# Half of a convolution as ScalarE products added by GpSimd, and three more weight blocks split

## The chip, the cores and the metric

One of the eight cores of a Trainium2 chip runs the program. The metric is the device time of one execution, in microseconds (us). The engines of the core work side by side, each through its own queue in order: TensorE (PE in the profile; its weight loads are PEld) multiplies matrices, VectorE (DVE) and ScalarE (ACT) work elementwise on tiles of 128 partitions, GpSimd (POOL) does small elementwise work and issues some transfers, and SyncE (SP) issues the large ones. SBUF holds 128 partitions of data, PSUM holds TensorE's results.

## The reference

A transformer of three layers on one sequence of 256 tokens, width 1024, all in float32. Two layers form the first block (attention mixers, a dense feed-forward and a mixture of experts). The second block, where the change lies, is:

```python
u = rms_norm(h, mix_norm_g)
proj = u @ w_in
q, k, v, glu_a, glu_g = split(proj)            # 512 columns each
attn_out = moba_attention(heads(q), heads(k), heads(v), rel_bias)
c = glu_a * sigmoid(glu_g)
c = depthwise_causal_conv(c, w_dw, taps=31) + b_dw
conv_out = silu(layer_norm(c) * ln_g + ln_b)
h = h + concat([attn_out, conv_out]) @ w_out
h = h + (silu(rms_norm(h) @ w_gate) * (rms_norm(h) @ w_up)) @ w_down
return rms_norm(h, final_norm_g)
```

With 256 tokens there is a single attention block, so attention is causal softmax attention over 256 keys with a bias by distance, eight heads of 64.

## The kernel before: how the work is laid out

The program is one long straight line in the order of the network. All weights stream in blocks of 1 MB, 128 partitions by 2048 columns, through the class `Stream`: a block is loaded into one of a few raw buffers by SyncE (`_load`, L81), and split into a high and a low part (`_split`, L93): ScalarE writes the rounded high part `wh` (L103), VectorE subtracts it from the raw values into `wl` (L104). A product then takes three passes of TensorE in the fast rounded format (`mm3`, L198): high by high, high by low, low by high. There are three raw and three split buffers here. A block whose number is in `native` is not split: TensorE multiplies the raw float32 values directly, which the profile shows as two matmul instructions for each product, and its raw buffer is held until TensorE has read it.

In the second block the ten blocks of `w_in2` are numbered from 0: blocks 0 to 3 hold the gated convolution input, 128 channels each (tile `ct`), with the gate beside its value; 4 and 5 are q, 6 and 7 are k, 8 and 9 are v. `NATIVE2` (L31) names the unsplit ones: 0, 1, 4, 5, 6 and 7. `proj_cols` (L281) computes a block with channels on the partitions, `proj_tok` (L306) with tokens on them.

The convolution (L1279 to L1302): for each of the four channel tiles ScalarE computes the sigmoid of the gate (L1281), VectorE multiplies (L1282) into `ug`. `conv(ct)` (L1292) starts the sum `cv` with the bias and the last tap on ScalarE (L1294) and adds the 30 other taps on VectorE, each a multiply by a weight per partition and an addition, over a shifted range of 226 to 255 columns (L1298):

```python
for j in range(30):
    back = 30 - j
    nc.vector.scalar_tensor_tensor(cv[:, ct, back:], ug[:, ct, :T - back], cw[:, ct, j:j + 1],
                                   cv[:, ct, back:], op0=ALU.mult, op1=ALU.add)
```

Attention runs in four steps (`STEPS`: two token halves, two groups of four heads). `scores` (L460): TensorE's products of q and k into two PSUM banks, on VectorE the bias and the row maximum (L481) and its negation (L483), on ScalarE the exponential with its sum (L485), on VectorE the reciprocal (L487), on ScalarE the scaling (L490). `values` (L495): transposes (L501), ScalarE copies (L504), the product with v, and the split of the result into `oT` (L204, L205). Each of the first two steps is followed by one block of v, whose PSUM bank (number 7) ScalarE empties (L1305).

After the last tap: the mean over channels by TensorE (`pmu`), VectorE's subtraction (L1326), ScalarE's square (L1327), the variance by TensorE (`pvr`, L1333), GpSimd's reciprocal root (`rstd_of`, L345), a product that spreads it over the partitions (`prs`), VectorE's multiplication (L1343), ScalarE's SiLU (L1345) and the split. The product with `w_out2` (four blocks) is cut into eight parts of 12 matmuls (token half by weight block, `Mix.part`, L527); the parts of blocks 2 and 3 need the convolution, those of 0 and 1 attention.

The order of each engine's queue is set when the program is built, by a planner: among the instructions whose inputs are ready by its own estimates it takes the one that stands first in the program, and `high_priority` sections ahead of the others. The splits of `w_in2` are such a section. `tc.issue_after(x)` keeps an instruction behind `x` in its engine's queue. On the chip each queue then runs in that fixed order, each instruction waiting for its semaphores. GpSimd also scales the factors of the next norm by 32 (`times32`, L231) and issues small loads (`load_small`, L215).

Of the kernel before, what the change touches and what calls it, by code (L numbers as in the profile page):

```python
# [10 lines left out]
F32 = mybir.dt.float32  # L11
# [4 lines left out]
AF = mybir.ActivationFunctionType  # L16
ALU = mybir.AluOpType
AX = mybir.AxisListType

P = 128  # L20
D = 1024
T = 256
# [5 lines left out]
NE = 8  # L28
R_RAW = 3
N_SPLIT = 3  # L30
NATIVE2 = (0, 1, 4, 5, 6, 7)  # L31


class Buffers:
# [109 lines left out]
def tile_model(ctx, tc, io, out):  # L144
    nc = tc.nc
# [22 lines left out]
    for i in range(len(steps_) + 1):  # L168
        if i < len(steps_):
            e, j = steps_[i]  # L170
            moe_order += [io[n][e][j][kh] for n in ("w1_m", "w3_m") for kh in range(2)]
        if i:
            e, j = steps_[i - 1]
# [107 lines left out]
    def proj_cols(xT, full=None, group="mm"):  # L281

        wh, wl = take8()
        o = bank(group, "pc")
        for ct in range(2):
            for k in range(8):
                oc = o[:, ct * 256:(ct + 1) * 256]
                if wl is None:
                    mm(oc, wh[:, k, tok(ct)], full[:, k, :], k == 0, k == 7)
                else:  # L290
                    mm3(oc, wh[:, k, tok(ct)], wl[:, k, tok(ct)], xT[0][:, k, :], xT[1][:, k, :], k == 0, k == 7)
        return o.rearrange("p (c t) -> p c t", c=2)
# [272 lines left out]
    xT = new_xT()  # L565
# [9 lines left out]
    with tc.tile_pool(name="l0", bufs=1) as lp:  # L575
# [6 lines left out]
        qT = lp.tile([P, 4, T], F32, tag="qT", name="qT")  # L582
        kT = lp.tile([P, 4, T], F32, tag="kT", name="kT")
        vb = lp.tile([P, 2, 512], F32, tag="vb", name="vb")
        with tc.tile_pool(name="gla", bufs=1) as gp:
# [35 lines left out]
            for tt in range(2):  # L621
# [3 lines left out]
                for q in range(2):  # L625
# [5 lines left out]
                    for j in range(2):  # L631
                        rl = g2([P, 2, 256], "rl")
                        nc.scalar.activation(rl[:, :, :S], pis[j][:, :, :S], AF.Relu)
                        for i in range(2):
# [3 lines left out]
                                                           op0=ALU.mult, op1=ALU.add)  # L638
                            first = False
                for r in range(8):  # L640
# [4 lines left out]
                                               op0=ALU.not_equal, op1=ALU.max)  # L645
# [76 lines left out]
            for tt in range(2):  # L722
# [13 lines left out]
                for h in range(4):  # L736
                    nc.vector.scalar_tensor_tensor(o_s[:, h, :], o_s[:, h, :], rs[:, h:h + 1], sg[:, tt, tok(h)],
                                                   op0=ALU.mult, op1=ALU.mult)
# [9 lines left out]
        with tc.tile_pool(name="t0", bufs=1) as tp, tc.tile_pool(name="t0w", bufs=2) as wo:  # L748
# [25 lines left out]
            xT = xT2  # L774
# [3 lines left out]
    with tc.tile_pool(name="f0", bufs=2) as fp, tc.tile_pool(name="f0r", bufs=4) as fr, tc.tile_pool(name="f0w", bufs=1) as fw:  # L778
# [13 lines left out]
        x, xT = xn, xT2  # L792
# [62 lines left out]
    with tc.tile_pool(name="l1", bufs=1) as lp:  # L855
# [6 lines left out]
        with tc.tile_pool(name="fox", bufs=1) as gp:  # L862
# [36 lines left out]
            qT = gp.tile([P, 4, T], F32, tag="qT", name="qT")  # L899
# [31 lines left out]
        with tc.tile_pool(name="t1", bufs=1) as tp, tc.tile_pool(name="t1w", bufs=1) as wo:  # L931
# [5 lines left out]
            copied, logits, xTf = [], [], []  # L937
# [47 lines left out]
    with tc.tile_pool(name="moer", bufs=4) as mr, tc.tile_pool(name="moe2", bufs=2) as m2:  # L985
# [229 lines left out]
        xT = new_xT()  # L1215
        xTf = xp.tile([P, 8, T], F32, tag="b8", name="xTf")
# [46 lines left out]
    with tc.tile_pool(name="s1", bufs=1) as lp:  # L1263
# [3 lines left out]
        cw = load_const(lp, "conv_w")  # L1267
        cpar = load_const(lp, "conv_p")
# [6 lines left out]
        ug = lp.tile([P, 4, T], F32, tag="ug", name="ug")  # L1275
        ga = lp.tile([P, 4, T], F32, tag="ga", name="ga")
        cv = lp.tile([P, 4, T], F32, tag="cv", name="cv")
        ws.first = True
        for ct in range(4):  # L1279
            o = convs[ct] if ct < 1 else proj_cols(xT, xTf)  # L1280
            nc.scalar.activation(ga[:, ct, :], o[:, 0, :], AF.Sigmoid)  # L1281
            nc.vector.tensor_tensor(ug[:, ct, :], ga[:, ct, :], o[:, 1, :], op=ALU.mult)  # L1282
        qT = lp.tile([P, 4, T], F32, tag="qT", name="qT")
        kT = lp.tile([P, 4, T], F32, tag="kT", name="kT")
        for i in range(2):
            nc.scalar.activation(qT[:, 2 * i:2 * i + 2, :], proj_cols(xT, xTf), AF.Copy, scale=0.125)
        for i in range(2):
            nc.scalar.activation(kT[:, 2 * i:2 * i + 2, :], proj_cols(xT, xTf), AF.Copy)
        v = lp.tile([P, 2, 512], F32, tag="v", name="v")
        scores, values = attention(t2, t2, qT, kT, v, lambda h: strip[:, h, :], None, oT, 0, on_act=True)  # L1290

        def conv(ct):  # L1292

            nc.scalar.activation(cv[:, ct, :], ug[:, ct, :], AF.Identity, bias=cpar[:, 0, ct:ct + 1],  # L1294
                                 scale=cw[:, ct, 30:31])
            for j in range(30):
                back = 30 - j
                nc.vector.scalar_tensor_tensor(cv[:, ct, back:], ug[:, ct, :T - back], cw[:, ct, j:j + 1],  # L1298
                                               cv[:, ct, back:], op0=ALU.mult, op1=ALU.add)

        for i, step in enumerate(STEPS):
            conv(i)  # L1302
            scores(*step)
            if i < 2:
                nc.scalar.activation(v[:, :, i * 256:(i + 1) * 256], proj_tok(xT, group="pj"), AF.Copy)  # L1305
            if i:
                values(*STEPS[i - 1])
        with tc.tile_pool(name="t2", bufs=1) as tp, tc.tile_pool(name="t2w", bufs=1) as wo:
# [3 lines left out]
            xT = new_xT()  # L1312
# [31 lines left out]
            for ct in range(4):  # L1344
                nc.scalar.activation(cv[:, ct, :], cv[:, ct, :], AF.Silu, bias=cpar[:, 2, ct:ct + 1],  # L1345
                                     scale=cpar[:, 1, ct:ct + 1])
# [159 lines left out]
```

## Time and profile before

| | |
|---|---|
| median of 3 runs | 1835.7 us (1832.89 to 1836.01) |
| the profiled execution | 1834.43 us |
| its span, first to last instruction | 1832.7 us |
| mean granted clock of TensorE, as a share of full speed | 0.987 |
| busy: PE, DVE, ACT, POOL | 1783.2, 1340.8, 1094.9, 93.9 us |

Times in the rows are microseconds from the span's start. In a timeline a row gives start, duration, engine, line, operation, the tile that it writes and those it reads, shapes, how many are merged (x54), and in brackets the idle time before it and what ended that. A duration runs from an instruction's start to its result; the next one can start before it ends, so for merged rows the time divided by the count is the spacing.

### The profile page before, as it was taken

What the parts mean: (1) busy time and instruction counts of PE and PEld (TensorE: products, weight loads), DVE (VectorE), ACT (ScalarE), POOL (GpSimd) and SP (SyncE); (2) the same over time, 40 slices, a digit from 0 to 9 for tenths busy, and PEclk for the clock granted to TensorE, in tenths of its full rate; (3) what the DMA queues carried; (4) which work ended last, traced back from release to release, by engine and by line L of the source; (5) the groups of instructions that cost most, each with busy time, mean ns of one, the idle gap of its engine ahead of it and who ended that gap; (6) DMA issues with size and microseconds to landing.
All of it is one profiled execution on the core that took longest, in us unless ns stands there. A gap on an engine that the chain in (4) does not pass through costs nothing. (4 is left out here: it accounts for less than half of the span.)

```text
span 1832.7 us, 24585 instructions
## 1 busy us (share of the span) xinstructions
PE 1783.2 (97%) x9903; PEld 1510.5 (82%) x9903; DVE 1340.8 (73%) x1365; ACT 1094.9 (60%) x1014; POOL 93.9 (5%) x136
## 2 busy tenths in 40 slices
PE   8999999999999999999999999999999989899998
PEld 7897999898778888888788788787887868789997
DVE  6856444545678888888888888888888978955443
ACT  5454433444567777777777777777777753564442
POOL 1101100010010000000000000000001022010000
PEclk9999999999989999999999999999999999999999
DMA  8453985263379999999999999999999924536530
GB/s 299 161 186 109 399 319 185 69 214 141 119 308 420 383 377 367 381 365 356 380 369 366 372 368 369 371 376 368 364 370 383 392 95 152 207 139 251 188 123 24
DMA packets 75418, 512.50 MB, mean 280 GB/s; under 512 B 8572, under 2 KB 8725, under 8 KB 17312
## 3 DMA queue, kind: packets, MB, share of 16 engines
q1 hardware_dynamic: 66240, 476.15, 68.1%
q0 software_dynamic: 8768, 34.17, 5.0%
q8 instruction: 80, 1.31, 0.3%
q10 hardware_dynamic: 288, 0.52, 0.1%
q14 instruction: 42, 0.34, 0.1%
HBM read 495.57 MB, written 19.96 MB: 281 GB/s over the span
## 5 line engine op out<-in xcount | busy, mean ns | idle before, releaser
L104 DVE TENSOR_TENSOR wl<-wraw,wh 128x2048 fp32r<-128x2048 f32 (+1 forms) x446 | 1012.0, 2286 | 302.4 <-ACT wh L103 300.3
L103 ACT ACTIVATE wh<-wraw 128x2048 fp32r<-128x2048 f32 (+1 forms) x446 | 851.9, 1912 | 467.8 <-issue 135.1
L196 PE MATMUL hh<-wl,eTh 128*128 128x512 f32 x896 | 355.9, 397 | 3.2 <-DVE wl L104 3.2
L196 PE MATMUL hh<-wh,eTh 128*128 128x512 f32 x896 | 355.2, 396 | 0.0
L196 PE MATMUL hh<-wh,eTl 128*128 128x512 f32 x896 | 353.3, 395 | 0.0
L196 PE MATMUL pc<-xTh,wh 128*128 128x256 f32 x944 | 270.6, 287 | 1.1 <-ACT xTh L204 1.1
L196 PE MATMUL pc<-xTl,wh 128*128 128x256 f32 x944 | 269.4, 285 | 0.9 <-DVE xTl L205 0.8
L196 PE MATMUL pc<-xTh,wl 128*128 128x256 f32 x944 | 269.2, 285 | 0.4 <-DVE wl L104 0.4
L196 PEld LDWEIGHTS hh<-wl,eTh 128*128 128x128 f32 x896 | 168.9, 188 | 46.1 <-DVE wl L104 7.8
L196 PEld LDWEIGHTS hh<-wh,eTh 128*128 128x128 f32 x896 | 168.8, 188 | 38.8 <-ACT eTh L204 0.2
L196 PEld LDWEIGHTS hh<-wh,eTl 128*128 128x128 f32 x896 | 168.8, 188 | 37.9
L196 PEld LDWEIGHTS pc<-xTh,wh 128*128 128x128 f32 x944 | 183.1, 194 | 4.3 <-ACT xTh L204 1.5
L196 PEld LDWEIGHTS pc<-xTl,wh 128*128 128x128 f32 x944 | 183.0, 194 | 2.2 <-DVE xTl L205 1.5
L196 PEld LDWEIGHTS pc<-xTh,wl 128*128 128x128 f32 x944 | 182.9, 194 | 0.7 <-DVE wl L104 0.6
L196 PE MATMUL acc<-wl,mah 128*128 128x512 f32 x448 | 180.8, 404 | 0.0
L196 PE MATMUL acc<-wh,mal 128*128 128x512 f32 x448 | 176.7, 395 | 0.3 <-DVE mal L205 0.3
L196 PE MATMUL acc<-wh,mah 128*128 128x512 f32 x448 | 163.5, 395 | 0.5 <-ACT mah L204 0.5
L196 PEld LDWEIGHTS acc<-wh,mah 128*128 128x128 f32 x448 | 84.4, 188 | 20.6 <-ACT mah L204 0.9
L196 PEld LDWEIGHTS acc<-wh,mal 128*128 128x128 f32 x448 | 84.6, 189 | 18.3 <-DVE mal L205 0.8
L196 PEld LDWEIGHTS acc<-wl,mah 128*128 128x128 f32 x448 | 84.4, 188 | 17.7
L196 PE MATMUL pt<-wh,xTh 128*128 128x256 f32 x256 | 74.7, 293 | 2.2 <-ACT v L1305 1.7
L196 PE MATMUL pt<-wl,xTh 128*128 128x256 f32 x256 | 73.5, 288 | 0.0
(338 smaller groups left out, 1865.7 us busy)
## 6 DMA issues: line engine op xcount, KB each, us to landing
wraw<-in_w_m_dram SPq DMA_DIRECT2D x336, 1024.0 KB, 7.2
wraw<-in_w_d_dram SPq DMA_DIRECT2D x33, 1024.0 KB, 5.6
wraw<-in_w_dram SPq DMA_DIRECT2D x33, 1024.0 KB, 4.8
wraw<-in_w_ab_dram SPq DMA_DIRECT2D x14, 1024.0 KB, 5.0
wraw<-in_w_cd_dram SPq DMA_DIRECT2D x12, 1024.0 KB, 4.8
wraw<-in_w_in_dram SPq DMA_DIRECT2D x10, 1024.0 KB, 5.4
xg_d<-zero POOLq DMA_DIRECT2D x8, 1024.0 KB, 44.8
rows<-scr POOLq DMA_DIRECT2D x3, 1536.0 KB, 11.1
```

The source lines that it names most:

```text
L103: self.last_split = (nc.scalar.activation(wh[:, c], raw[:, c], AF.Copy), nc.vector.tensor_tensor(wl[:, c], raw[:, c], wh[:, c].bitcast(F32 ...
L104: nc.vector.tensor_tensor(wl[:, c], raw[:, c], wh[:, c].bitcast(F32), op=ALU.subtract))
L196: return nc.tensor.matmul(o, l, r, start=start, stop=stop, skip_group_check=True)
```

## The change

Three blocks (5, 6 and 7: the second of q, both of k) leave `NATIVE2` and are split like the others. The first term of the convolution is issued for each channel tile right behind its gate product. Channel tiles 0 and 1 are convolved by ScalarE, which writes each tap's product to one of seven buffers, and GpSimd, which adds it to the sum; tiles 2 and 3 stay on VectorE, ahead of the first two attention steps. The products of tile 1 are kept behind ScalarE's q copies in part: taps 14 to 21 behind the first, 22 to 29 behind the second.

```diff
-NATIVE2 = (0, 1, 4, 5, 6, 7)
+NATIVE2 = (0, 1, 4)
...
             nc.vector.tensor_tensor(ug[:, ct, :], ga[:, ct, :], o[:, 1, :], op=ALU.mult)
+            nc.scalar.activation(cv[:, ct, :], ug[:, ct, :], AF.Identity, bias=cpar[:, 0, ct:ct + 1],
+                                 scale=cw[:, ct, 30:31])
+
+        def conv(ct, on_pool, between=()):
+            for j in range(30):
+                back = 30 - j
+                if on_pool:
+                    p = lp.tile([P, T], F32, tag="tap", name="tap", bufs=7)
+                    i = len(between) + (j - 30) // 8
+                    with tc.issue_after(between[i].ins) if i >= 0 and between else ExitStack():
+                        nc.scalar.activation(p[:, back:], ug[:, ct, :T - back], AF.Copy, scale=cw[:, ct, j:j + 1])
+                    nc.gpsimd.tensor_tensor(cv[:, ct, back:], cv[:, ct, back:], p[:, back:], op=ALU.add)
+                else:
+                    nc.vector.scalar_tensor_tensor(cv[:, ct, back:], ug[:, ct, :T - back], cw[:, ct, j:j + 1],
+                                                   cv[:, ct, back:], op0=ALU.mult, op1=ALU.add)
+
+        conv(0, True)
         qT = lp.tile([P, 4, T], F32, tag="qT", name="qT")
         kT = lp.tile([P, 4, T], F32, tag="kT", name="kT")
-        for i in range(2):
-            nc.scalar.activation(qT[:, 2 * i:2 * i + 2, :], proj_cols(xT, xTf), AF.Copy, scale=0.125)
+        copies = [nc.scalar.activation(qT[:, 2 * i:2 * i + 2, :], proj_cols(xT, xTf), AF.Copy, scale=0.125)
+                  for i in range(2)]
+        conv(1, True, copies)
...
-        def conv(ct):
-
-            nc.scalar.activation(cv[:, ct, :], ug[:, ct, :], AF.Identity, bias=cpar[:, 0, ct:ct + 1],
-                                 scale=cw[:, ct, 30:31])
-            for j in range(30):
-                back = 30 - j
-                nc.vector.scalar_tensor_tensor(cv[:, ct, back:], ug[:, ct, :T - back], cw[:, ct, j:j + 1],
-                                               cv[:, ct, back:], op0=ALU.mult, op1=ALU.add)
-
         for i, step in enumerate(STEPS):
-            conv(i)
+            if i < 2:
+                conv(2 + i, False)
             scores(*step)
```

## Rows read from the trace of the kernel before

**Rows 1.** The page: busy tenths of TensorE in 40 slices of the span.

```profile
PE   8999999999999999999999999999999989899998
```

**Rows 2.** Windows: length, PE, PEld, DVE, ACT, POOL busy (instructions), granted clock, DMA share, GB/s.

```profile
1541.00:1572.00 31.00, 31.00 (x158) 27.56 (x157) 31.00 (x78) 6.46 (x7) 0.00 (x0) 1.00 0.35 123
1572.00:1595.00 23.00, 17.48 (x127) 16.00 (x126) 22.05 (x53) 16.45 (x35) 0.00 (x0) 0.92 0.68 248
```

**Rows 3.** Timeline of VectorE: taps of the convolution, and two weight splits.

```profile
1546.09 20.60 DVE L1298 SCALAR_TENSOR_TENSOR cv<-ug,conv_w,cv 128x249 f32<-128x249 f32 x54
...
1582.47 4.49 DVE L104 TENSOR_TENSOR wl<-wraw,wh 128x2048 fp32r<-128x2048 f32 x2
...
1587.56 6.14 DVE L1298 SCALAR_TENSOR_TENSOR cv<-ug,conv_w,cv 128x244 f32<-128x244 f32 x12
```

**Rows 4.** Timeline of TensorE: projections, scores, values' input, first mean.

```profile
1532.73 0.47 PE L196 MATMUL pc<-xTh,wh 128*128 128x256 f32 x1
...
1544.42 15.92 PE L196 MATMUL pc<-xTf,wraw 128*128 128x256 f32 x73
...
1572.15 0.71 PE L196 MATMUL lg<-kT,qT 64*128 64x128 f32 x8
...
1581.67 1.62 PE L196 MATMUL lg<-kT,qT 64*128 64x256 f32 x8 [1.72 <-DVE mx L481]
1584.98 0.58 PE L196 MATMUL pt<-wh,xTh 128*128 128x256 f32 x1 [1.69 <-ACT v L1305]
...
1587.70 0.38 PE L196 MATMUL pt<-wh,xTh 128*128 128x256 f32 x1
...
1594.81 1.19 PE L196 MATMUL pmu<-cv,c 128*128 128x256 f32 x2 [2.10 <-issue]
```

**Rows 5.** Timeline of ScalarE: first term of tile 2, a weight conversion, two scaled copies.

```profile
1540.20 0.60 ACT L1294 ACTIVATE cv<-ug,conv_p,conv_w 128x256 f32<-128x256 f32 x1 [0.95 <-DVE ug L1282]
...
1563.41 1.91 ACT L103 ACTIVATE wh<-wraw 128x2048 fp32r<-128x2048 f32 x1 [4.38 <-DMA wraw<-in_w_in_dram]
...
1602.44 0.90 ACT L490 ACTIVATE z<-z,rsm 128x256 f32<-128x256 f32 x2
```

**Rows 6.** Timeline of VectorE and GpSimd round GpSimd's widest product of two tensors.

```profile
72.77 2.29 DVE L104 TENSOR_TENSOR wl<-wraw,wh 128x2048 fp32r<-128x2048 f32 x1 [3.46 <-ACT wh L103]
...
73.30 3.96 POOL L666 TENSOR_TENSOR sg<-sg,gnorm 128x1024 f32<-128x1024 f32 x1 [25.35 <-ACT sg L664]
...
76.14 1.28 DVE L688 TENSOR_TENSOR QK<-E,kaT 128x128 f32<-128x128 f32 x1 [1.08 <-ACT E L683]
...
77.34 0.28 DVE L689 TENSOR_TENSOR QK<-E,qaT 128x128 f32<-128x128 f32 x1
```

**Rows 7.** Timelines of GpSimd and VectorE round two one-column operations.

```profile
1627.39 0.23 POOL L351 TENSOR_SCALAR rs_v<-ss 128x1 f32<-128x1 f32 x1 [19.24 <-ACT u L388]
...
1637.04 1.88 POOL L351 TENSOR_SCALAR rs_v<-ss 128x1 f32<-128x1 f32 x1 [7.37 <-ACT u L388]
...
1636.55 2.28 DVE L104 TENSOR_TENSOR wl<-wraw,wh 128x2048 fp32r<-128x2048 f32 x1
```

**Rows 8.** Timelines of GpSimd and VectorE round a scaling with one input.

```profile
1469.08 2.80 POOL L232 TENSOR_SCALAR lnp<-lnp 128x1024 f32<-128x1024 f32 x1 [63.16 <-DMA lnp<-in_ln_g_dram]
...
1469.85 2.42 DVE L104 TENSOR_TENSOR wl<-wraw,wh 128x2048 fp32r<-128x2048 f32 x1
```

**Rows 9.** Timeline of GpSimd: its last work before the convolution's end.

```profile
1526.43 3.78 POOL L232 TENSOR_SCALAR ffng<-ffng 128x1024 f32<-128x1024 f32 x1 [3.50 <-DMA ffng<-in_ffn_g_dram]
```

**Rows 10.** Timelines of TensorE and ScalarE: variance, first convolution tile converted, end of mixing.

```profile
1605.03 1.84 PE L196 MATMUL pvr<-c,ga 128*128 128x1 f32 x16
...
1614.97 0.41 ACT L204 ACTIVATE oTh<-cv 128x256 fp32r<-128x256 f32 x1
...
1633.77 0.39 PE L196 MATMUL acc<-wl,oTh 128*128 128x512 f32 x1
1634.00 0.39 PE L196 MATMUL acc<-wh,oTl 128*128 128x512 f32 x1
```

## The prediction

> **What bounds the kernel now.** I read the page's slices first [rows 1]: TensorE is busy nine tenths or more in 36 of the 40 slices (45.8 us each) and dips in the first, the last, number 33, ahead of the second block, and number 35, 1558 to 1604 us, in that block's attention and convolution. All that the change edits runs between 1517 and 1634, so I cut out the two stretches round that dip [rows 2]. From 1541 to 1572 TensorE is busy all the time and so is VectorE; from 1572 to 1595 TensorE works 17.5 of 23 us at a lower mean clock, while VectorE still works 22. GpSimd does nothing in both, ScalarE 6.5 + 16.5 of 54 us.
>
> VectorE's timeline [rows 3] shows why: the 120 taps of the convolution end at 1593.7 (1587.56 + 6.14), and weight splits stand between them (two take 4.49 us, one [rows 6] 2.29, so 2.2 apart). 54 taps take 20.60 us, 0.381 each. The attention's maxima have to be fitted in there. TensorE's timeline [rows 4] gives the price: it stands 1.72 us for the scores' maxima, 1.69 us for ScalarE's copy of v, 2.10 us before the first mean of the convolution, together 5.5 us, and after the second stop 12 starts take 2.72 us (1584.98 to 1587.70), 0.227 each, where the split blocks' 96 take 11.69 (1532.73 to 1544.42), 0.122: the lower of the two clock levels, 1.2 us lost. So 6.7 us at most can be won there, and what the projections give.
>
> **The projections.** Four blocks computed from unsplit weights (each 32 matmuls) run from 1544.42 to 1572.15, 6.93 us each; the two split blocks before them (48 matmuls each) run from 1532.73 to 1544.42, 5.85 us each [rows 4]. Three more split blocks save 3 x 1.08 = 3.3 us of TensorE on the path. They add three conversions on ScalarE (1.91 us) and three subtractions on VectorE (2.2) [rows 3, 5, 6]. The transfers move too: in the kernel before the raw buffer of such a block is free only when TensorE has read it; now it is free after the split, so the loads of the last blocks and of the output weights are issued earlier on SP's queue. I cost that at nothing: TensorE reaches blocks 5, 6 and 7 at about 1551, 1557 and 1563, and their splits can run some 5 us ahead. If the splits come late, each costs up to 1.91 + 2.29 us.
>
> **What leaves VectorE.** 60 taps x 0.381 = 22.9 us. The four first terms (tap 30 with the bias) already run right behind the gate product, so putting them first in the program moves nothing.
>
> **What ScalarE gets.** 60 products of 226 to 255 columns. The nearest row is its copy with a scale per partition: two of 128x256 take 0.90 us, 0.45 each, 0.42 for 240 columns [rows 5]. The other end is the 0.60 us of the activation with bias and scale [rows 5]: 25 to 36 us in all; I take 0.42, since that row has the same form, 25 us. With the splits that is 31 us more on an engine that is idle 31 of the 54 us of [rows 2] and more before, so the room is there. But a product waits until one of seven buffers is given back by an addition, and behind it in ScalarE's queue stand the copies of q, k and v and the weight conversions. Eight products wait for each of the two q copies, by the program.
>
> **What GpSimd gets.** 60 additions of about 240 columns. GpSimd adds none this wide in the trace. The nearest row is its product of two tensors, 128x1024 in 3.96 us [rows 6]. As it stands, that is 0.93 us for 240 columns, and 1.16 with the 0.23 us that a one-column operation takes [rows 7]. But the row holds a wait: a VectorE subtraction with both inputs in SBUF ran from 72.77 to 75.06. From there to GpSimd's end at 77.26 are 2.20 us, or 0.52 for 240 columns; with half of the 0.23 for what does not grow with the columns, 0.65. I take that, since it fits the rows of the next part too; the ends are 0.52 and 1.16, so 31 to 70 us in all, 39 as taken, if nothing is in the way. GpSimd's own queue holds little else: the scaling of the next norm's factors [rows 9], which VectorE needs only after 1627, and the root of the variance, which follows the additions anyway.
>
> **The two engines against each other.** While GpSimd ran that product, a VectorE multiply of two SBUF operands begun at 76.14 took 1.28 us; its successors of the same shape take 0.28 [rows 6]. It finished 0.16 us after GpSimd. The other way round, a one-column GpSimd operation begun at 1637.04 took 1.88 us, against 0.23 ten us before, and ended at 1638.92, right behind a subtraction of VectorE that ended at 1638.83 [rows 7]. So an operation of VectorE on two SBUF tensors and one of GpSimd exclude each other while they read. VectorE's tap reads both its tensors from SBUF, and so does GpSimd's addition. The hold of one 1024-column product is 75.06 to 77.14 (77.42 less 0.28), 2.08 us, so 0.49 us for 240 columns.
>
> A one-input scaling by GpSimd of 2.80 us delayed the VectorE subtraction that began 0.77 us into it by only 0.13 us (2.42 instead of 2.29) [rows 8]: here the hold was about 0.9 us, shorter than the instruction. The Trainium skill (SBUF — State Buffer, section "SBUF: two separate sides") says that the pair of ports is locked for the whole instruction and the loser fully blocks. By that rule each addition would hold 0.65 us, and the sum below would be 48 x 0.16 = 7.7 us larger; the scaling's row disagrees with that.
>
> **The sum.** GpSimd is free for additions from about 1530.2, after that scaling [rows 9]. Until VectorE's first tap of channel tile 2 (its first term ends at 1540.8 [rows 5]) there are 10.6 us, less one split of 2.2: 12 additions of 0.65, and 48 are left. In the kernel before, 99 taps (37.7 us) and five splits (11.0) stand in VectorE's timeline from 1540.8 to 1593.7, of which [rows 3] show the longest run and the last; they leave 4.2 us for the gate and attention. From 1540.8 VectorE now has 60 taps (22.9), eight splits (three new ones and those five: 17.7) and the 4.2: 44.8 us, alone done at 1585.6. The 48 holds add 23.5 us, less the 4.2 in which VectorE has at most one operand in SBUF: 19.3. The convolution ends at 1604.9, 11.2 us later than now.
>
> What is that worth? From the last tap to the first converted convolution tile the chain takes 1614.97 - 1593.7 = 21.3 us [rows 3, 10], in part because attention's work stands between its steps in the same queues. Its second part, from the variance's matmuls, takes 9.9 [rows 10]; with at least 3 us for mean, subtraction and square before it (an estimate) it can shrink to 13. Then TensorE has the four convolution parts of the output product left, 48 matmuls 0.23 us apart [rows 10], 11 us. So the mixing ends at 1604.9 + 13 + 11 = 1628.9 at the earliest, against 1634.4 now, or at 1637.2 if the chain is as long as it is. I take the long chain, since the second half of attention still stands in the same queues and its maxima also wait on VectorE: +2.8 us; and 2 us for matmuls at the lower clock after a longer stop (1.2 of them as in [rows 4]): **+5 us**. The profiled execution took 1834.43 us (span 1832.7 and 1.7 around it), 1.3 below the median of the runs; on the median that is 1841.
>
> **Rivals.**
> *Faster.* VectorE's relief counts and the exclusion costs little. The point that decides is the hold: with less than (1593.7 - 1540.8 - 44.8 + 4.2) / 48 = 0.26 us per addition the convolution ends no later than now. Then TensorE keeps the 3.3 us of the projections and some of the 6.7 us of stops: -3.3 to -10, say -6.5, 1829. For it: the scaling's short hold, and the short chain above, which gives -5 even with the exclusion. Against it: the 1.28 us row.
> *ScalarE's queue.* GpSimd and VectorE in turn need 0.49 + 0.38 = 0.87 us per addition; with five splits 48 additions take 51 us, 1.06 each. The last product waits for addition 52, at about 1583. If the copy of k is queued behind it (the program puts it there), the scores that need k wait until 1583 instead of being ready at 1569, and TensorE stands 14 us rather than 5.5. With the convolution's delay behind it: about +12, 1848. For it: a product can never be more than seven additions ahead. Against it: the planner may put the copies ahead of the last products, and ScalarE has 31 idle us to catch up in.
> *No difference.* The 3.3 us of the projections and the later convolution cancel: 1835.7 with 0.2% (3.7 us) to either side, about what a measurement of this kernel can tell from no change.
>
> **Chances.** Forecast (+3.7 to +10) 0.35, ScalarE's queue (+10 to +18) 0.18, no difference 0.18, faster 0.29. That is slower 0.53, same 0.18, faster 0.29. The range for 8 in 10 goes from 1828, most of the faster case, to 1853, the upper bound of the queue's case. The forecast's own range is 1839 to 1846.
>
> **What would show it.** Right: GpSimd's additions have a mean well above 0.65 us from 1541 on and near 0.65 before; the taps on VectorE are then 0.8 us or more apart and 0.38 when GpSimd is idle; the last tap or addition ends near 1605; TensorE's idle time before the means of the convolution grows. Three split blocks take 17.5 instead of 20.8 us. Wrong: additions of 0.65 us all along with taps 0.38 apart; the convolution over before 1594; or ScalarE waiting for GpSimd's buffers with TensorE idle before the first scores, which is the second rival.

## The result, and the profile after

The changed kernel takes 1856.6 us (median of 4 runs, 1851.7 to 1861.2) against 1835.5 of the kernel before beside it: the ratio is 1.0113, with a 95% interval of 1.0090 to 1.0135, some 21 us more. The profiled execution took 1851.67 us, with a span of 1849.9 against 1832.7.

The page's slices of the changed kernel, which answer to [rows 1]:

```profile
PE   8999999999999999999999999999999988599998
POOL 1101100100010000000000000000001128310000
```

Slice 35 falls from 8 to 5, just after the ones in which GpSimd is busy. The windows of the same stretches as in [rows 2], and the next one (columns as there):

```profile
1541.00:1572.00 31.00, 25.81 (x188) 24.57 (x186) 26.11 (x28) 21.65 (x40) 28.65 (x32) 1.00 0.38 136
1572.00:1595.00 23.00, 9.26 (x56) 8.86 (x56) 23.00 (x31) 12.29 (x18) 15.68 (x19) 0.63 0.25 81
1595.00:1612.00 17.00, 10.70 (x64) 9.95 (x66) 13.48 (x37) 11.83 (x28) 0.00 (x0) 0.70 0.58 202
```

TensorE works 9 of the 23 us from 1572 on, at a mean granted clock of 0.63 instead of 0.92, and VectorE is still busy for all of them, although half of the taps have left it. TensorE's timeline, against [rows 4]:

```profile
1562.10 0.39 PE L196 MATMUL pc<-xTh,wl 128*128 128x256 f32 x1 [1.07 <-DVE wl L104]
...
1567.60 0.28 PE L196 MATMUL pc<-xTh,wl 128*128 128x256 f32 x1
1584.27 1.22 PE L196 MATMUL lg<-kT,qT 64*128 64x128 f32 x8 [16.39 <-POOL cv L1296]
...
1586.01 0.41 PE L196 MATMUL pt<-wh,xTl 128*128 128x256 f32 x1
1586.22 0.41 PE L196 MATMUL pt<-wh,xTh 128*128 128x256 f32 x1
...
1597.83 1.19 PE L196 MATMUL lg<-kT,qT 64*128 64x128 f32 x4 [4.30 <-DVE mx L481]
1601.61 1.22 PE L196 MATMUL lg<-kT,qT 64*128 64x128 f32 x4 [2.59 <-DVE mx L481]
1603.71 0.58 PE L196 MATMUL pt<-wh,xTh 128*128 128x256 f32 x1 [0.89 <-ACT v L1317]
...
1614.11 0.67 PE L196 MATMUL pmu<-cv,c 128*128 128x256 f32 x2 [1.32 <-issue]
```

Up to the first mean its stops add up to 26.6 us, where [rows 4] have 5.5. The largest, 16.4 us, stands ahead of the first scores; after it matmuls start 0.21 us apart, 0.12 at full clock: the lower of the two clock levels. ScalarE's timeline tells what the scores waited for:

```profile
1541.64 1.90 ACT L103 ACTIVATE wh<-wraw 128x2048 fp32r<-128x2048 f32 x1
1543.44 0.36 ACT L1281 ACTIVATE ga<-pc 128x256 f32<-128x256 f32 x1
...
1564.25 0.49 ACT L1295 ACTIVATE tap<-ug,conv_w 128x234 f32<-128x234 f32 x1 [0.30 <-POOL cv L1296]
1565.05 0.49 ACT L1295 ACTIVATE tap<-ug,conv_w 128x235 f32<-128x235 f32 x1 [0.31 <-POOL cv L1296]
...
1583.17 0.51 ACT L1295 ACTIVATE tap<-ug,conv_w 128x255 f32<-128x255 f32 x1 [0.33 <-POOL cv L1296]
1583.59 0.58 ACT L1308 ACTIVATE kT<-pc 128x512 f32<-128x512 f32 x1
```

The first copy of k runs right behind the last product, and each product (tap) waits for an addition of GpSimd that gives a buffer back. VectorE's timeline, against [rows 3]:

```profile
1549.60 2.22 DVE L1298 SCALAR_TENSOR_TENSOR cv<-ug,conv_w,cv 128x226 f32<-128x226 f32 x3
...
1561.97 16.24 DVE L1298 SCALAR_TENSOR_TENSOR cv<-ug,conv_w,cv 128x232 f32<-128x232 f32 x20
...
1591.49 2.79 DVE L1298 SCALAR_TENSOR_TENSOR cv<-ug,conv_w,cv 128x247 f32<-128x247 f32 x7
1594.20 0.28 DVE L481 CUSTOM_DVE_ANT_0 z<-lg,strip 128x128 f32<-128x128 f32 x1
...
1607.39 1.00 DVE L1298 SCALAR_TENSOR_TENSOR cv<-ug,conv_w,cv 128x254 f32<-128x254 f32 x2
```

While GpSimd adds, 20 taps take 16.24 us, 0.81 each; once it is done, 7 take 2.79, 0.40 each (0.381 in [rows 3]). Its additions, in GpSimd's timeline, end at 1589.1, just before that change of pace:

```profile
1527.33 2.16 POOL L1296 TENSOR_TENSOR cv<-cv,tap 128x226 f32<-128x226 f32 x3 [4.19 <-ACT tap L1295]
1533.12 55.97 POOL L1296 TENSOR_TENSOR cv<-cv,tap 128x229 f32<-128x229 f32 x57
```

The stretch begins at a different moment in each execution, so later comparisons count from its first weight split. In the kernel before that is 1525.27; VectorE's timeline there also shows the nine taps that it did at once:

```profile
1525.27 2.29 DVE L104 TENSOR_TENSOR wl<-wraw,wh 128x2048 fp32r<-128x2048 f32 x1 [1.11 <-ACT wh L103]
...
1529.04 4.41 DVE L1298 SCALAR_TENSOR_TENSOR cv<-ug,conv_w,cv 128x226 f32<-128x226 f32 x9 [0.67 <-ACT cv L1294]
```

In the changed kernel it is 1523.06. So the first mean comes 91.1 us after it instead of 69.5: 21.5 us more. TensorE's stops make 21.1 of that (26.6 less 5.5). The projections end 2.1 us earlier by the same measure, that is 3.1 earlier but for the 1.07 us wait. The remaining 3.6 is work that takes longer: the two blocks of v, in which 37 starts (22 from 1585.80 on, 15 from 1604.09 on) are 0.09 us further apart at the lower clock, against 12 in [rows 4], so 25 x 0.09 = 2.3 us; and the scores between them, some 1.2 us.

### The profile page after: what moved, and what is told of

Its sections match the earlier page's. It is cut to its first block, busy times and chain, and to the rows that moved or that the text cites. A ratio compares the mean times of both kernels' runs of the same rounds, so it can differ in the third digit from the quotient of the medians.

```text
span 1849.9 us, 24805 instructions
## 1 busy us (share of the span) xinstructions
PE 1780.4 (96%) x9951; PEld 1510.7 (82%) x9951; DVE 1342.1 (73%) x1308; ACT 1125.8 (61%) x1077; POOL 148.1 (8%) x196
## 5 line engine op out<-in xcount | busy, mean ns | idle before, releaser
L196 PE MATMUL pc<-xTh,wh 128*128 128x256 f32 x992 | 283.6, 286 | 0.9 <-ACT xTh L204 0.9
L196 PE MATMUL pc<-xTh,wl 128*128 128x256 f32 x992 | 282.2, 284 | 1.1 <-DVE wl L104 1.1
L196 PE MATMUL pc<-xTl,wh 128*128 128x256 f32 x992 | 282.3, 285 | 0.8 <-DVE xTl L205 0.8
L196 PEld LDWEIGHTS pc<-xTh,wh 128*128 128x128 f32 x992 | 191.5, 193 | 3.8 <-ACT xTh L204 1.3
L196 PEld LDWEIGHTS pc<-xTl,wh 128*128 128x128 f32 x992 | 191.4, 193 | 2.2 <-DVE xTl L205 1.4
L196 PEld LDWEIGHTS pc<-xTh,wl 128*128 128x128 f32 x992 | 191.4, 193 | 1.4 <-DVE wl L104 1.3
```

The costliest lines, as they stand in the source:

```text
L196: return nc.tensor.matmul(o, l, r, start=start, stop=stop, skip_group_check=True)
```

## The experiments

Two theories stood against each other. **Holds:** GpSimd's additions and VectorE's taps exclude each other, so VectorE is late with everything. **Queue:** ScalarE waits for GpSimd's buffers, and what stands behind the products waits with it. Ratios are to the kernel before, run beside each, with their 95% intervals. The indented texts are what was expected before each run; they name kernels by labels, which stand in brackets behind the results here. Where they say port theory, that is the holds.

**One part at a time.** The splits alone, in the kernel before:

```diff
-NATIVE2 = (0, 1, 4, 5, 6, 7)
+NATIVE2 = (0, 1, 4)
```

> The kernel before with three more blocks split, and nothing else. Port theory (taps of VectorE and additions of GpSimd exclude each other) and queue theory (ScalarE's copies of k stand behind products that GpSimd releases) both say that this part costs little: TensorE saves 3.3 us in the projections, VectorE gets 6.6 us of splits, so -3 to +5 us against the kernel before. Rival: the late splits and late loads make the loss; then +10 us or more.

1840.8 us, 1.0026 (1.0009 to 1.0043) [e1_split_only], as both expected. The other part alone, the changed kernel with the blocks unsplit as before:

```diff
-NATIVE2 = (0, 1, 4)
+NATIVE2 = (0, 1, 4, 5, 6, 7)
```

> The change with the six unsplit blocks of the kernel before: the convolution's part alone. Port and queue theory: +13 to +24 us, with TensorE idle 12 us or more before the first scores. Rival (splits): under +8 us.

1853.5 us, 1.0098 (1.0072 to 1.0124) [e2_pool_only]. Nearly all of the loss belongs to the convolution. The place was only half as expected, by TensorE's timeline:

```profile
1579.88 1.23 PE L196 MATMUL lg<-kT,qT 64*128 64x128 f32 x8 [8.32 <-POOL cv L1296]
1593.41 0.58 PE L196 MATMUL pt<-wl,xTh 128*128 128x256 f32 x1 [11.79 <-DVE wl L104]
```

It stands 8.3 us before the first scores, not 12, and then 11.8 for a weight split that VectorE does late. Then the convolution's halves. GpSimd's additions left out but for the last of each tile, the products kept (that half of the convolution is not summed):

```diff
-                    nc.gpsimd.tensor_tensor(cv[:, ct, back:], cv[:, ct, back:], p[:, back:], op=ALU.add)
+                    if j == 29:
+                        nc.gpsimd.tensor_tensor(cv[:, ct, back:], cv[:, ct, back:], p[:, back:], op=ALU.add)
```

> GpSimd's additions are left out except the last of each tile (58 of 60; the sum of that half of the convolution is not computed); ScalarE's 60 products stay. Both theories, queue and holds, have GpSimd as the cause and expect all of the loss back and the relief of VectorE besides: taps 0.38 apart, no stop of TensorE over 3 us before the first scores, 1826 to 1835. If instead ScalarE's own work (60 products of 0.4 us and three conversions) is the cause, the time stays above 1843.

1833.3 us, 0.9985 (0.9973 to 0.9998) [e7_no_add]. ScalarE's 60 products and the splits cost nothing in this company: the additions are the whole loss. It also bounds the gain: with half of the convolution's sums for free, 0.15% is all that VectorE's relief and the three splits together bring. VectorE's timeline of this kernel:

```profile
1559.21 8.07 DVE L1299 SCALAR_TENSOR_TENSOR cv<-ug,conv_w,cv 128x232 f32<-128x232 f32 x20
...
1578.65 0.28 DVE L481 CUSTOM_DVE_ANT_0 z<-lg,strip 128x128 f32<-128x128 f32 x1
```

The same 20 taps that took 16.24 us beside additions take 8.07, 0.40 each.

**The holds.** VectorE's taps of tiles 2 and 3 accumulate in a PSUM bank, and only the last writes SBUF, so that a tap reads one tensor from SBUF instead of two:

```diff
...
+                    acc_ = cvp[:, ct - 2, back:]
-                    nc.vector.scalar_tensor_tensor(cv[:, ct, back:], ug[:, ct, :T - back], cw[:, ct, j:j + 1],
-                                                   cv[:, ct, back:], op0=ALU.mult, op1=ALU.add)
+                    nc.vector.scalar_tensor_tensor(cv[:, ct, back:] if j == 29 else acc_, ug[:, ct, :T - back],
+                                                   cw[:, ct, j:j + 1], acc_, op0=ALU.mult, op1=ALU.add)
```

> The change with VectorE's taps of tiles 2 and 3 accumulated in PSUM, the last one written to SBUF: each tap then reads one SBUF tensor. Port theory: the taps are 0.38 to 0.45 us apart instead of 0.81 while GpSimd adds, and the first maxima follow the scores at once, near 1586 instead of 1594; the time falls by 6 to 12 us. Queue theory: GpSimd's additions alone are 0.77 us apart, so the first scores still start near 1584 after 14 to 17 us of idle time. If the taps stay 0.8 us apart, the port is not what spaces them.

1852.5 us, 1.0084 (1.0056 to 1.0112) [e4_psum]. VectorE's timeline of this kernel, the first row beside additions, the second after them:

```profile
1563.99 7.54 DVE L1302 SCALAR_TENSOR_TENSOR cvp<-ug,conv_w,cvp 128x231 f32<-128x231 f32 x15
...
1608.87 3.00 DVE L1302 SCALAR_TENSOR_TENSOR cvp<-ug,conv_w,cvp 128x238 f32<-128x238 f32 x6
```

0.50 us each in both, a little above the 0.38 to 0.45 expected. So taps with one SBUF input are not held; PSUM costs 0.12 us more per tap and removes the hold. (That they also write PSUM is not the reason: the last tap of tile 2, which writes SBUF, takes 0.48 us at 1590.82, while GpSimd still adds.) Yet the time falls by less than the intervals can tell, and TensorE's timeline shows why:

```profile
1591.56 1.23 PE L196 MATMUL lg<-kT,qT 64*128 64x128 f32 x8 [19.77 <-POOL cv L1299]
```

The scores still wait for the copies of k.

**The queue.** The copies of k ahead of tile 1's last products:

```diff
+        copies += [nc.scalar.activation(kT[:, 2 * i:2 * i + 2, :], proj_cols(xT, xTf), AF.Copy) for i in range(2)]
         conv(1, True, copies)
-        for i in range(2):
-            nc.scalar.activation(kT[:, 2 * i:2 * i + 2, :], proj_cols(xT, xTf), AF.Copy)
```

> The change with the copies of k ahead of the second channel tile's products: the products wait in eights for the two q and the two k copies. Queue theory: the first scores start near 1569 instead of 1584 us, TensorE's 16.4 us of idle time before them go, and the time is at most 8 us above the kernel before. Port theory: the first maxima on VectorE still come after 1585, since the taps ahead of them are 0.8 us apart, TensorE waits for them instead, and the time stays 12 us or more above.

1859.7 us, 1.0126 (1.0098 to 1.0154) [e3_k_first]: no gain. TensorE's timeline:

```profile
1577.39 1.23 PE L196 MATMUL lg<-kT,qT 64*128 64x128 f32 x8 [3.27 <-POOL cv L1296]
1587.24 0.58 PE L196 MATMUL pt<-wl,xTh 128*128 128x256 f32 x1 [8.12 <-DVE wl L104]
1598.80 0.76 PE L196 MATMUL lg<-kT,qT 64*128 64x128 f32 x2 [4.40 <-DVE mx L481]
1602.19 1.22 PE L196 MATMUL lg<-kT,qT 64*128 64x128 f32 x6 [2.63 <-DVE mx L481]
1611.18 1.14 PE L501 MATMUL ppt<-ident,z 128*128 128x128 f32 x3 [7.76 <-ACT z L490]
```

The 16 us came back in pieces, for VectorE's split and maxima and for ScalarE's scaling of the exponentials. Either the holds hid the gain, or the queue hands its wait on. To see the queue by itself, VectorE's taps of tiles 2 and 3 were left out but for the last of each (that half is not computed), so that nothing can be held:

```diff
-                else:
+                elif j == 29:
                     nc.vector.scalar_tensor_tensor(cv[:, ct, back:], ug[:, ct, :T - back], cw[:, ct, j:j + 1],
...
```

> VectorE's taps of channel tiles 2 and 3 are left out except the last of each (58 of 60; that half of the convolution is not computed), GpSimd's additions and ScalarE's products are as in the changed kernel. No tap can be held any more and VectorE has 22 us less to do than even by the diff. If holds of the taps were what cost, the time falls to 1832 or below. If ScalarE's queue behind GpSimd is enough by itself, TensorE still stands 10 us or more before the first scores and the time stays at 1843 or above. GpSimd's additions: 0.77 us apart if the taps don't slow them, with the gaps of the weight subtractions left.

1843.3 us, 1.0044 (1.0026 to 1.0061) [e6_no_taps]. ScalarE's timeline of this kernel, two products and the first copy of k:

```profile
1568.64 0.49 ACT L1295 ACTIVATE tap<-ug,conv_w 128x235 f32<-128x235 f32 x1 [0.26 <-POOL cv L1296]
1569.39 0.49 ACT L1295 ACTIVATE tap<-ug,conv_w 128x236 f32<-128x236 f32 x1 [0.26 <-POOL cv L1296]
...
1587.14 0.58 ACT L1308 ACTIVATE kT<-pc 128x512 f32<-128x512 f32 x1
```

and TensorE's:

```profile
1587.82 1.23 PE L196 MATMUL lg<-kT,qT 64*128 64x128 f32 x8 [18.44 <-issue]
```

The releaser here is given only as "issue", but ScalarE's first copy of k ended 0.1 us earlier. So the queue alone makes an 18 us stop, and a slower kernel even with 58 taps fewer. The same pair of columns (235, 236) is 0.80 us apart in the changed kernel and 0.75 here: a tap beside it costs an addition 0.05 us, while the addition costs the tap 0.43.

With the copies of k moved forward in this kernel:

> e6_no_taps (VectorE's taps of tiles 2 and 3 left out but for the last of each, so nothing is held) with the copies of k ahead of the second tile's last eight products and of those that the program ties to them. If TensorE's 18.4 us stop before the first scores is nothing but the copies' place in ScalarE's queue, it shrinks to about the 6.4 us of e5_k_first_psum, and the time falls from 1843 to 1832 to 1838. If everything else that stands behind the products (weight conversions, exponentials) is then as late, TensorE's stops before the second scores or the first transposes grow by what was won and the time stays at 1841 or above.

1848.1 us, 1.0075 (1.0050 to 1.0101) [e12_no_taps_k_first]. TensorE's timeline:

```profile
1573.27 1.22 PE L196 MATMUL lg<-kT,qT 64*128 64x128 f32 x8 [6.78 <-POOL cv L1296]
1587.05 2.56 PE L196 MATMUL lg<-kT,qT 64*128 64x256 f32 x8 [5.04 <-DVE mx L481]
1593.58 0.77 PE L501 MATMUL ppt<-ident,z 128*128 128x128 f32 x2 [3.97 <-ACT z L490]
```

The first stop shrank as expected, and the wait went on to the next things in the queue: reordering does not help. More buffers for the products instead, again without the taps (bfloat16, so that 15 fit: the products are rounded):

```diff
-                    p = lp.tile([P, T], F32, tag="tap", name="tap", bufs=7)
+                    p = lp.tile([P, T], BF16, tag="tap", name="tap", bufs=15)
```

> e6_no_taps (VectorE's taps of tiles 2 and 3 left out but for the last of each) with 15 buffers for the products instead of 7, in bfloat16 so that they fit (the products are rounded). If ScalarE's queue stands because a product can be only as many additions ahead as there are buffers, the last product waits for the addition eight places earlier, 8 x 0.77 + one weight subtraction of 2.2 = about 8 us: the copies of k run some 8 us earlier and TensorE's stop before the first scores falls from 18.4 to about 10 us, and since nothing is put in the copies' place (unlike in e12_no_taps_k_first) the time falls too, by 3 to 8 us, to 1835 to 1840. If the queue does not come from the buffers, neither moves. GpSimd's additions may take another time with one bfloat16 input; the stop is then to be read against 8 additions of that time.

1837.5 us, 1.0015 (1.0002 to 1.0029) [e14_no_taps_ring15], and the stop halves. TensorE's timeline:

```profile
1575.44 1.23 PE L196 MATMUL lg<-kT,qT 64*128 64x128 f32 x8 [8.77 <-issue]
```

9.7 us less, where about 8 were worked out; but not all of that is the ring of buffers. In this execution GpSimd's long run of additions began 2.5 us earlier, 10.2 us after the first weight split instead of 12.7 (it stands behind the scaling of [rows 9], which waits for its load), and with a bfloat16 input the additions are 0.72 us apart instead of 0.77, some 2.2 us over 42 of them. Eight additions fewer to wait for make 8 x 0.77 = 6.2. Together that is 10.9; the rest lies in weight splits and conversions that fall otherwise. That the ring is what makes products wait can be counted in the traces: with 7 buffers no product begins before the addition seven places earlier has ended, and 33 of 53 begin 0.03 us after it; with 15 buffers the same holds for fifteen places (18 of 45).

**Both at once, and each alone, in the whole convolution.** First the copies of k forward plus PSUM:

> Both edits of the two kernels e3_k_first and e4_psum at once: the copies of k ahead of the second tile's last products, and VectorE's taps with their sum in PSUM. If the loss is the sum of two separate causes (k behind products, taps held by additions), each edit alone can have been hidden by the other, and both together bring most of it back: TensorE stands less than 5 us before the first scores, 1838 to 1843. If the queue is a general one (whatever stands behind the products on ScalarE waits as long as GpSimd adds, up to about 1590), the wait only moves on to the next thing behind the products, the weight conversions and the exponentials: TensorE stands 10 us or more after the first scores and the time stays at 1848 or above.

1847.5 us, 1.0058 (1.0037 to 1.0078) [e5_k_first_psum], between the two and nearer to the rival: TensorE stops 6.4, 1.9 and 7.7 us before scores. Then PSUM plus 15 buffers, and 15 buffers alone, which make a square with the changed kernel and the one in PSUM above:

> e4_psum (all taps computed, VectorE's in PSUM) with 15 product buffers in bfloat16: both causes reduced at once with the order of the program left as it is. TensorE's stop of 19.8 us before the first scores falls to 10 to 12, and the time from 1851 to 1842 to 1847. If the copies of k were not what the time hung on, it stays at 1849 or above.

> The changed kernel with 15 product buffers in bfloat16 and nothing else: the taps of VectorE stay in SBUF and are held. Against e15_psum_ring15 (1838, 1.0017) it gives the price of the holds once the queue is short, against the changed kernel (1.0113) the price of the queue. If the holds cost time on their own, the taps stay 0.81 us apart, the convolution ends 8 us or more later than in e15_psum_ring15, and the time is 1843 to 1850. If with the short queue the holds are hidden, 1840 or below.

1838.0 us, 1.0017 (1.0003 to 1.0031) [e15_psum_ring15], better than expected, and 1850.8 us, 1.0082 (1.0065 to 1.0099) [e16_ring15], just above the 1843 to 1850 expected for holds that cost on their own. One sign of it missed: with 15 buffers alone the convolution ends 80.8 us after the first weight split, not later than with both (83.7). VectorE's timeline has the first maximum, in the kernel with 15 buffers alone:

```profile
1594.11 0.28 DVE L481 CUSTOM_DVE_ANT_0 z<-lg,strip 128x128 f32<-128x128 f32 x1
```

and in the one with both:

```profile
1580.08 0.28 DVE L481 CUSTOM_DVE_ANT_0 z<-lg,strip 128x128 f32<-128x128 f32 x1
```

Counted from the first weight split of each:

| kernel | ratio | first scores (TensorE) | first maximum (VectorE) | TensorE's stops up to the first mean |
|---|---|---|---|---|
| before | 1 | 46.9 us | 50.7 us | 5.5 us |
| changed | 1.0113 | 61.2 | 71.1 | 26.6 |
| taps in PSUM | 1.0084 | 63.3 | 64.5 | 21.9 |
| 15 buffers | 1.0082 | 51.7 | 66.7 | 22.1 |
| both | 1.0017 | 52.0 | 54.3 | 11.1 |
| copies of k ahead, taps in PSUM | 1.0058 | 49.9 | 54.0 | 16.6 |

The first maximum needs two things: scores, which wait for ScalarE's queue, and VectorE, on which 47 taps stand ahead of it in the changed kernel, 40 of them held (3 + 7 + 20 + 10 in its timeline). Whoever mends one waits for the other: 6.6 us and 4.4 us alone, 16.8 together. The two single ratios overlap with that of the changed kernel, and only the pair stands clear of it.

Two things qualify this. In the kernels with PSUM the order of VectorE's queue is another too: 31 taps stand ahead of the first maximum, not 47. That 47 do no harm when nothing holds them is shown by the kernel without additions, where they stand ahead of it as well and it comes 49.7 us after the first split (1578.65 less 1528.96), and no product waits there either; holds and order were not parted any further. And the first maximum alone does not give the time: in the last row it comes as early as in the row above, while TensorE's later stops are longer and the ratio is 1.0058. The stops of the last column follow the ratios.

With the three blocks unsplit besides:

> e15_psum_ring15 with the three projection blocks unsplit as in the kernel before: TensorE has 3.3 us more to do, VectorE three subtractions (6.6 us) less, and GpSimd, which stands during each of them, is done some 6 us earlier. By e1_split_only and e11_twelve_split the splits cost more than they bring here: 1834 to 1838. If they bring their 3.3 us once the two causes are gone, 1840 to 1842.

1835.3 us, 1.0002 (0.9991 to 1.0013) [e17_psum_ring15_unsplit]: the same as before, no better. In TensorE's timeline the stop before the first scores is gone; they come 46.9 us after the first split (1529.30), as in the kernel before:

```profile
1576.18 0.71 PE L196 MATMUL lg<-kT,qT 64*128 64x128 f32 x8
```

**Fewer additions.** Tile 0 alone on GpSimd, blocks unsplit:

```diff
-        conv(1, True, copies)
...
-            if i < 2:
-                conv(2 + i, False)
+            if i < 3:
+                conv(1 + i, False)
```

> Only channel tile 0 goes to ScalarE and GpSimd, tiles 1 to 3 stay on VectorE, and the three projection blocks are unsplit as in the kernel before. GpSimd is done 30 additions after its start near 1531, at about 1531 + 30 x 0.77 + four weight subtractions of 2.2 = 1563, before the copies of k are due. By the queue theory TensorE has then no long stop before the first scores. By the holds, some 20 of VectorE's 90 taps are held 0.43 us each, 8.6 us, against 11.4 us that it is relieved of: the convolution ends within 3 us of before. Both together: 1833 to 1838, no change that counts. If the loss is in proportion to the additions whatever their place, half of 21 us, about 1846.

1844.2 us, 1.0052 (1.0033 to 1.0071) [e8_one_tile]: slower than expected. GpSimd was done at 1556.7 and the copies of k were in time, as expected, but TensorE stands elsewhere, by its timeline:

```profile
1579.22 0.58 PE L196 MATMUL pt<-wl,xTh 128*128 128x256 f32 x1 [8.45 <-DVE wl L104]
```

VectorE's timeline of this kernel, up to that split:

```profile
1538.17 5.58 DVE L1298 SCALAR_TENSOR_TENSOR cv<-ug,conv_w,cv 128x226 f32<-128x226 f32 x7 [2.03 <-ACT cv L1283]
...
1544.00 11.31 DVE L1298 SCALAR_TENSOR_TENSOR cv<-ug,conv_w,cv 128x233 f32<-128x233 f32 x14
...
1555.56 21.40 DVE L1298 SCALAR_TENSOR_TENSOR cv<-ug,conv_w,cv 128x241 f32<-128x241 f32 x53
1576.88 2.28 DVE L104 TENSOR_TENSOR wl<-wraw,wh 128x2048 fp32r<-128x2048 f32 x1
```

The order of VectorE's queue is fixed when the kernel is built. A weight split stands behind 53 taps in a row, so what the 21 taps before them lost (7 in 5.58 us and 14 in 11.31, 0.80 each; 21 x 0.42 = 8.8 us) delays it, and TensorE stands 8.45 us for it. (The expectation below counts 19 of these taps.) The test is the same kernel with the sums of tile 1 in PSUM:

> e8_one_tile, with the 30 taps of tile 1, which run while GpSimd adds tile 0, summed in PSUM instead of SBUF, so that each tap reads one tensor from SBUF. In e8_one_tile 19 such taps were 0.81 us apart and the weight split that stands behind them on VectorE came late, with TensorE idle 8.5 us for it. If the exclusion of two SBUF readers is the cause, these taps are 0.50 us apart (as in e4_psum), that split comes some 5 us earlier, TensorE's stop for it is under 5 us, and the time falls by 3 to 6 us to 1838 to 1841. If the stop has another cause (the order in which VectorE's queue was built, the raw weights landing late), it stays at 8 us or more and so does the time, 1844.

1842.8 us, 1.0033 (1.0020 to 1.0046) [e9_one_tile_psum]. In TensorE's timeline the stop for that split is 3.0 us, as expected; the gain in time is inside the intervals and smaller than expected:

```profile
1579.86 0.39 PE L196 MATMUL pt<-wl,xTh 128*128 128x256 f32 x1 [3.00 <-DVE wl L104]
```

Last, only the first 12 taps of tile 0 on GpSimd, without and with the three split blocks:

```diff
-        conv(0, True)
+        conv(0, True, range(12))
...
+            ct = (1, 0, 2, 3)[i]
+            conv(ct, False, range(0 if ct else 12, 30))
```

> Only the first 12 taps of channel tile 0 go to ScalarE and GpSimd, where VectorE has little to do yet; the other 18 and tiles 1 to 3 stay on VectorE, the projection blocks as before. GpSimd is done about 12 x 0.77 + 2.8 us after its start near 1528, at 1540 to 1543. If the loss comes only from additions beside VectorE's taps, a few taps are held (at most 6 x 0.43 = 2.6 us) and VectorE is relieved of 4.6: no stop for a weight split over 2 us, 1832 to 1837. If each addition costs in proportion (21 us / 60), +4 us, 1841.

> e10_twelve with the three projection blocks split as in the changed kernel. TensorE saves up to 3.3 us on the projections and VectorE has three splits of 2.2 us more, against 4.6 us of taps less. By e1_split_only (splits alone: 1.0026 of before) and e10_twelve the two add up: within 4 us of before, 1833 to 1840. This is the version that could beat both kernels; it does if the relief lets the splits come in time, below 1833.

1841.9 us, 1.0033 (1.0021 to 1.0045) [e10_twelve], and 1847.4 us, 1.0055 (1.0040 to 1.0070) [e11_twelve_split]: both missed. The first has the number of a cost in proportion to the additions, but no tap was held here. VectorE's timeline of it has another wait:

```profile
1542.49 3.82 DVE L1296 SCALAR_TENSOR_TENSOR cv<-ug,conv_w,cv 128x238 f32<-128x238 f32 x10 [6.39 <-POOL cv L1294]
```

In its order tile 0's other 18 taps come first and wait for GpSimd's sum. By the same point of the stretch (19.6 us after the first weight split) the kernel before had begun 32 taps; here VectorE has begun none, and GpSimd has added 12. No complete version beat it.

## Why the prediction was right or wrong

The direction was right, but mostly for another reason than the sum gives; the forecast of 1841 us was 15.6 us short, and the range, which ended at 1853, missed the result by 3.6. The step that failed by most is that the sum has no term for TensorE standing before the first scores: that wait stood among the rivals as an alternative, and it measured 16.4 us.

**Right, by its own steps.** The projections: 3.3 us worked out, 3.1 measured. ScalarE's product: 0.42 us, and four in a row take 1.63 (ScalarE's timeline from 1534.26 on), 0.41. The hold: 0.49, measured 0.43; the pair of a tap and an addition 0.87, measured 0.81. The addition: 0.65 taken, 0.75 to 0.77 measured, inside the ends. The rule of the Trainium skill (SBUF — State Buffer, section "SBUF: two separate sides"), that the pair of ports is locked for the whole instruction and the loser fully blocks, would make the pair of tap and addition 0.38 + 0.75 = 1.13 us apart; the trace has 0.81, so it disagrees. The same section of the Trainium skill names two SBUF inputs of VectorE as a case that contends; the taps in PSUM, which have one, take 0.50 us beside additions and without them, which agrees.

**The first step that failed: where VectorE's taps begin.** The sum lets them start at 1540.8, when the gate of tile 2 was ready before. They began at 1549.60, or 1551.8 on the old clock (2.2 us are the earlier start of the stretch). The gate's sigmoid at 1543.44 stands behind products that wait for buffers and a weight conversion behind them. That tiles 0 and 1, whose inputs come first, are the ones that leave VectorE was in the sum; that VectorE then has little to do until the later gates come, and begins 11 us later, was not. The convolution ends at 1608.4, 1610.6 on the old clock, where 1604.9 was forecast.

**The second: what the delay is worth.** It was priced at the end of the convolution, 2.8 us, with 2 us of lower clock. The loss lay before that: 16.4 us ahead of the first scores and 6.9 for the maxima (4.30 + 2.59). The convolution's end is not what the time hangs on: with both mends it comes 83.7 us after the first weight split, 15.3 later than in the kernel before, and the ratio is 1.0017. The second rival, ScalarE's queue, named the place, the cause and the size (14 us against 16.4), and got a chance of 0.18; its price of 12 us has VectorE's delay only at the convolution's end, and nothing for the maxima. Its time of 1583 has two slips: with seven buffers the last product waits for addition 53, not 52, and 48 additions at 0.87 us with five splits of 2.2 are 52.8 us, not 51. Put right, it is about 1586; the last product began at 1583.17, or 1585.4 on the old clock.

**The third, which made both too small: the cases were taken as alternatives.** Holds and queue are not two ways in which it could go. They feed the same step, the first maximum, from two sides, and both happened. The text had both halves and did not price them together.

The argument that the planner might put the copies of k ahead of the products was wrong for this kernel, and beside the point: with the copies ahead the wait went on to the next in the queue.

What stays open: with 15 buffers and the three blocks split TensorE still stands 8.2 to 8.8 us before the first scores; unsplit it does not. A deeper ring, and 15 buffers without the rounding, were not tried.

## What to carry to other kernels

Work given to an idle engine is worth no more than the wait that it ends, and it brings its own: before moving it, list what stands behind its producer in that queue and which other engine's work its consumer holds up, and price these together if they meet at one step. A ring of n buffers lets an in-order producer run n consumers ahead and then stops everything behind it; reordering that queue only chooses who waits. When a mend brings nothing, try it together with the other one before dropping it.

## What the runs showed that was not expected

A tap and an addition do not simply take turns: beside each other they come 0.81 us apart, where 0.38 and 0.75 would add up to 1.13. Nearly all of the loss is VectorE's (0.43 us; the addition loses 0.05). The longer subtraction of the weight split does stop GpSimd: with the taps left out, 57 additions took 57.14 us (GpSimd's timeline of that kernel), 14.4 more than 57 x 0.75; six such splits fall wholly into that time and two in part, so it is some 2 us each, of 2.29 (an estimate). So each weight split that the change adds also delays the additions: with the three blocks unsplit the 57 took 47.98 us instead of 55.97. And a tap that accumulates in PSUM takes 0.50 us instead of 0.38, whether GpSimd adds or not.
